# The up projection of a ConvFFN as seven block products instead of eight, in a pass of its own

## Chip, core and metric

The kernel runs on one core of a Trainium2 chip. The metric is the device time of one execution in microseconds (us): 2776.97 us is the median of three runs before the change (2772.65 to 2777.08).

## What is computed

One layer over 512 latent tokens and 256 context tokens, width 2048: sandwich norms, a token mixer (mLSTM heads and differential attention) and a gated ConvFFN. The change sits in the ConvFFN, whose hidden width is 5632:

```python
def dwconv3(a, w, b):
    ap = jnp.pad(a, ((0, 0), (1, 1), (0, 0)))
    return ap[:, :-2] * w[0] + ap[:, 1:-1] * w[1] + ap[:, 2:] * w[2] + b

def conv_ffn(h, w_up, conv_w, conv_b, w_down):
    u = dwconv3(h @ w_up, conv_w, conv_b)
    gate, val = jnp.split(u, 2, axis=-1)
    return (jax.nn.silu(gate) * val) @ w_down

h_lat = modulate(rmsnorm(x, g_pre_ffn[l]), sh2, sc2)
x = x + ga2 * rmsnorm(conv_ffn(h_lat, ...), g_post_ffn[l])
```

`h` is 512 x 2048, `w_up` 2048 x 11264, `w_down` 5632 x 2048, all in float32.

## The kernel before, in words

Every large product is done in three passes on rounded operands. `split` (L127) makes `hi` (a copy rounded to fp32r, on ScalarE) and `lo` (source minus `hi`, on VectorE); `mm3` (L131) adds hi·hi, hi·lo and lo·hi in PSUM. Weights stream from DRAM through `load_w` (L100): each 128 x 2048 weight tile comes in two 512 KB transfers to `raw` (three buffers), and is split in four pieces of 512 columns into `whi`/`wlo` (four buffers each).

Up projection: `up(m)` (L1013) computes one tile of 128 hidden columns for all 512 tokens: 16 blocks of the inner dimension times three passes, 48 matmuls of 512 columns, weights stationary, the normalized tokens (`hhi`, `hlo`) moving. `up(2f)` is the gate, `up(2f+1)` the value of hidden tile f; 44 tiles f in all. `conv3` (L570) evaluates the width-3 convolution (one ScalarE and two VectorE operations), ScalarE does the SiLU, VectorE the product.

Down projection: after every four tiles f, `nat_group` (L886) multiplies the four gated tiles (split into `fhi`, `flo`) with 512 rows of `w_down` and adds the result to the 16 accumulators `y` on VectorE: 192 matmuls of 512 columns a group, 11 groups. The last group goes through `nat_last` (L891), one token block at a time, each followed by its norm and output (`post`).

Between the mixer and the FFN stands a transition (L976 to L1000): the last group of the mixer's output projection gives `y` token block by token block, `post` normalizes it, TensorE transposes it (`xt`), ScalarE modulates it into `hf`, and VectorE writes `hhi` (L999) and `hlo` (L1000). Half of the first up tile (256 tokens) is computed early, inside the transition.

`step` (L341) does a slice of the conditioning product (`wmB` weights against a vector, on VectorE, and 8 matmuls of one column named `modr` per 512 outputs); the FFN calls it 16 times.

The program is written in the order of the stages; a scheduler places each engine's instructions, and each engine then runs its own list in order. SP issues the loads from DRAM, POOL the stores to it.

Of the kernel before, what the change touches and what calls it, by code (L numbers as in the profile page):

```python
# [6 lines left out]
F32 = mybir.dt.float32  # L7
F32R = mybir.dt.float32r
AF = mybir.ActivationFunctionType
ALU = mybir.AluOpType  # L10
# [4 lines left out]
P = 128  # L15
D = 2048
KT = 16
TL = 512
# [4 lines left out]
NFF = DFF // P  # L23
# [35 lines left out]
class Prog:  # L59
# [7 lines left out]
    def mm(self, *a, **k):  # L67
        return self.pe(self.nc.tensor.matmul(*a, **k))  # L68
# [28 lines left out]
    def slot(self, name, dt=F32):  # L97
        return self.p_slot.tile([P, 512], dt, tag="slot", name=name)

    def load_w(self, src, n, act=False):  # L100

        his, los = [], []
        if act:
            bh, bl = self.act("wact"), self.act("wact")
        for j in range(n // 512):
# [16 lines left out]
        return get  # L122

    def act(self, name):
        return self.p_act.tile([P, 4, 512], F32R, tag="act", name=name)

# [4 lines left out]
    def mm3(self, ps, whi, wlo, ahi, alo, start, stop):  # L131
        mm = self.mm
        mm(ps, whi, ahi, start=start, stop=False)
        mm(ps, whi, alo, start=False, stop=False)
        mm(ps, wlo, ahi, start=False, stop=stop)


    def setup(self, ctx):
# [744 lines left out]
        else:  # L883
            nc.vector.tensor_tensor(y[tt][cc], ps, y[tt][cc], ALU.add)  # L884

    def nat_group(self, wsrc, acts, y, first, pool, tag):  # L886
# [21 lines left out]
        self.nc.scalar.activation(self.junk5(), t, AF.Square, accum_out=ss[:, cc:cc + 1])  # L908

    def junk5(self):  # L910
        return self.p_x.tile([P, 512], F32, tag="junk5", name="junk5", bufs=2)

    def stat_done(self, ss):
        r = self.p_s.tile([P, 1], F32, tag="rs1", name="rs1")
# [4 lines left out]
    def load_row(self, g):  # L919
        out = []  # L920
        for cc in range(4):
            t = self.p_x.tile([P, 512], F32, tag="row", name="row", bufs=4)
            self.nc.sync.dma_start(t, self.gg_d[g:g + 1, cc * 512:(cc + 1) * 512].broadcast_to([P, 512]))
            out.append(t)
        return out

    def new_ss(self):
        return self.p_s.tile([P, 4], F32, tag="ss4", name="ss4", bufs=4)
# [16 lines left out]
    def phase_out(self):  # L945
        nc, I = self.nc, self.I
        y = self.y
        self.x1_d = self.dram.tile([4, P, D], F32, name="x1_d")
        rows = []
        acts = self.mix_acts(3)  # L950
        ssy = [self.new_ss() for _ in range(4)]

        def each(tt, cc):
            self.stat(ssy[tt], cc, y[tt][cc])
            nc.vector.tensor_tensor(y[tt][cc], y[tt][cc], rows[cc], ALU.mult)  # L955

        def post(tt):
            r = self.stat_done(ssy[tt])
            ss = self.p_s.tile([P, 4], F32, tag="ssx", name="ssx")
            xs = []  # L960
            for cc in range(4):
                xn = self.p_x.tile([P, 512], F32, tag="xn", name="xn", bufs=8)
                cs = slice(cc * 512, (cc + 1) * 512)
                nc.sync.dma_start(xn, I["xn"][tt, :, cs])
# [12 lines left out]
        self.nat_last(lambda cc: I["wo"][cc, 3], acts, y, self.ps_mm, "mm", 3, each, post)  # L977
        self.ah = [self.act("hhi") for _ in range(4)]
        self.al = [self.act("hlo") for _ in range(4)]
        for tt in range(4):  # L980
            if tt == 2:
                self.early = self.up_mm(0, 0, 256)
            ts = slice(tt * P, (tt + 1) * P)
            for cc in range(4):
# [6 lines left out]
                hf = self.p_x.tile([P, 512], F32, tag="hf", name="hf", bufs=4)  # L991
                for j in range(4):
                    k = cc * 4 + j
                    js = slice(j * P, (j + 1) * P)
                    sh, sc = self.mcol[:, 16 + k:17 + k], self.mcol[:, 32 + k:33 + k]
                    nc.scalar.activation(hf[:, js], pt[:, js], AF.Identity, bias=sh, scale=sc)  # L996
                h3 = hf.rearrange("p (a b) -> p a b", b=P)
# [5 lines left out]
    def up_mm(self, m, t0, t1, part=None):  # L1003

        if part is None:
            part = (self.load_w(self.I["wu"][m], 2048), self.ps_mm.tile([P, 512], F32, tag="mm", name="mm"))
        get, ps = part
        for kt in range(KT):
            hi, lo = self.hl(kt)
            self.mm3(ps[:, t0:t1], *get(kt * P, P), hi[:, t0:t1], lo[:, t0:t1], kt == 0, kt == KT - 1)  # L1010
        return part

    def up(self, m):  # L1013
        ps = (self.up_mm(m, 256, TL, self.early) if m == 0 else self.up_mm(m, 0, TL))[1]
        u = self.p_x.tile([P, 512], F32, tag="u", name="u", bufs=4)
        c = self.cff.rearrange("p (a b) -> p a b", b=4)
        self.conv3(u, ps, c[:, m, :], TL)
        if m >= 12:
            self.step(64)
        return u  # L1020

    def phase_ffn(self):
        nc, I = self.nc, self.I
# [8 lines left out]
        def post(tt):  # L1032
            r = self.stat_done(ssy[tt])
            for cc in range(4):
# [3 lines left out]
                nc.vector.scalar_tensor_tensor(x1, y[tt][cc], r, x1, ALU.mult, ALU.add)  # L1038
                nc.sync.dma_start(self.out[tt, :, cs], x1)

        NG = NFF // 4
        for g in range(NG):
            acts = ([], [])
            for j in range(4):
                f = g * 4 + j
# [4 lines left out]
                hi = self.slot("fhi", F32R)  # L1050
                lo = self.slot("flo", F32R)
                self.split(hi, lo, u)
                acts[0].append(hi)
                acts[1].append(lo)
            if g == NG - 1:
                rows += self.load_row(1)
                self.nat_last(lambda cc: I["wd"][g, cc], acts, y, self.ps_sm, "sm", 4, each, post)
            else:
                self.nat_group(lambda cc: I["wd"][g, cc], acts, y, g == 0, self.ps_sm, "sm")

    def build(self):
        with ExitStack() as ctx:
            self.setup(ctx)
            self.phase_in()
            self.p_x = ctx.enter_context(self.tc.tile_pool(name="ext", bufs=2))
            self.cff = self.p_x.tile([P, 88 * 4], F32, name="cff", bufs=1)
            self.nc.sync.dma_start(self.cff, self.I["cff"])
            self.phase_out()
            self.phase_ffn()
# [100 lines left out]
```

## Time and profile before

| | us |
|---|---|
| median of three runs | 2776.97 |
| the profiled execution's own time | 2775.6 |
| its span (first to last instruction) | 2773.8 |
| end of the last VectorE statement chain of the mixer's output (last `xn`) | 1309.83 |
| up and down products without a break on TensorE | from 1325.46 |

A span is the time from the first to the last instruction of the trace; the execution's own time is 1.8 us longer. Engine names: PE is TensorE, PEld its weight loads, DVE VectorE, ACT ScalarE, POOL GpSimd, SP the queue that issues loads. A matmul's own duration in the trace holds its way through the array, which overlaps with its successor; the cost of one in a stream is the distance between two starts.

### The profile page before, as it was taken

The numbers are of one execution on the slowest core, as the hardware profiler recorded it, in microseconds if no ns is written. First come the engines' busy times: TensorE is split into PE (matmuls) and PEld (weight loads), VectorE is DVE, ScalarE is ACT, GpSimd is POOL, SyncE is SP. The second block draws the span as 40 slices with busy tenths as digits, with TensorE's granted clock in tenths as the row PEclk, the third lists the DMA queues.
The fourth block names the chain that finished last, engine by engine and source line by source line (L and its number), as shares of the span: only waits on it lengthen the run. The fifth ranks groups of instructions, "written<-read, shape, count | busy, mean of one in ns | idle before, by whom it ended". The sixth has DMA issues, their size and how long they took to land.

```text
span 2773.8 us, 35993 instructions
## 1 busy us (share of the span) xinstructions
PE 2714.9 (98%) x13796; PEld 2263.1 (82%) x13796; DVE 1603.4 (58%) x2938; ACT 1012.5 (37%) x1939; POOL 78.7 (3%) x101
## 2 busy tenths in 40 slices
PE   6999999999999999998999999999999999999998
PEld 3678899888888888887888888888888888888886
DVE  6585867776666666457535565544444444444446
ACT  4242444434334344526433232323232322323233
POOL 0000000000000000002000000000000000000000
PEclk9999999999999999999999999999999999999999
DMA  7875434333433433334224354422222232222225
GB/s 277 272 245 194 134 115 134 134 125 114 130 129 126 136 119 130 133 115 143 99 97 141 127 190 137 144 96 94 99 95 97 90 106 92 99 99 99 92 99 174
DMA packets 111963, 365.46 MB, mean 132 GB/s; under 512 B 12896, under 2 KB 13312, under 8 KB 111792
## 3 DMA queue, kind: packets, MB, share of 16 engines
q1 hardware_dynamic: 108144, 352.03, 37.9%
q0 software_dynamic: 3648, 11.14, 1.1%
q8 instruction: 108, 1.77, 0.3%
q14 instruction: 63, 0.52, 0.1%
HBM read 348.36 MB, written 14.76 MB: 131 GB/s over the span
## 4 chain that ended last, share of the span: by engine, by line
PE 51%; DVE 2%; ACT 1%; issue 0%; DMA 0%; POOL 0%; POOLq 0%; DVEq 0%; ACTq 0%
PE mm L68 34%; PE nat L68 16%; ACT junk L908 0%; DVE x L1038 0%; DVE y L884 0%; DVE y L1030 0%; DVE xn L965 0%; DMA raw<-in_wd 0%; POOL rs L174 0%; ACT hf L996 0%; DVE hlo L1000 0%; DVE wact L129 0%; DVE y L955 0%; PE modr L68 0%; ACT y L972 0%
## 5 line engine op out<-in xcount | busy, mean ns | idle before, releaser
L128 ACT CAST whi<-raw 128x512 fp32r<-128x512 f32 x792 | 490.0, 622 | 1149.7 <-PE mm L68 600.7
L129 DVE TENSOR_TENSOR wlo<-raw,whi 128x512 fp32r<-128x512 f32 x792 | 542.9, 689 | 602.0 <-ACT whi L128 597.5
L68 PE MATMUL mm<-hhi,whi 128*128 128x512 f32 (+1 forms) x1424 | 552.2, 388 | 3.8 <-DVE hhi L999 3.8
L68 PE MATMUL mm<-hhi,wlo 128*128 128x512 f32 (+1 forms) x1424 | 551.7, 387 | 0.8 <-DVE wlo L129 0.8
L68 PE MATMUL mm<-hlo,whi 128*128 128x512 f32 (+1 forms) x1424 | 551.8, 387 | 0.5 <-DVE hlo L1000 0.3
L68 PE MATMUL mm<-lhi,whi 128*128 128x512 f32 x912 | 373.4, 410 | 1.7 <-ACT whi L128 1.4
L68 PE MATMUL mm<-llo,whi 128*128 128x512 f32 x912 | 360.2, 395 | 0.0
L68 PE MATMUL mm<-lhi,wlo 128*128 128x512 f32 x912 | 359.9, 395 | 0.0
L68 PEld LDWEIGHTS mm<-hhi,whi 128*128 128x128 f32 x1424 | 268.0, 188 | 58.6 <-DVE hhi L999 4.2
L68 PEld LDWEIGHTS mm<-hhi,wlo 128*128 128x128 f32 x1424 | 268.0, 188 | 55.3 <-DVE wlo L129 1.0
L68 PEld LDWEIGHTS mm<-hlo,whi 128*128 128x128 f32 x1424 | 268.0, 188 | 54.9 <-DVE hlo L1000 1.0
L68 PE MATMUL nat<-whi,flo 128*128 128x512 f32 x640 | 249.7, 390 | 0.0
L68 PE MATMUL nat<-wlo,fhi 128*128 128x512 f32 x640 | 249.5, 390 | 0.0
L68 PE MATMUL nat<-whi,fhi 128*128 128x512 f32 x640 | 248.8, 391 | 0.0
L884 DVE TENSOR_TENSOR y<-nat,y 128x512 f32<-128x512 f32 x208 | 141.9, 688 | 179.5 <-PE nat L68 179.3
L254 DVE SCALAR_TENSOR_TENSOR macc<-raw,c,macc 128x512 f32<-128x512 f32 x240 | 179.5, 748 | 103.0 <-DMA raw<-in_wmB 100.2
L68 PEld LDWEIGHTS mm<-lhi,wlo 128*128 128x128 f32 x912 | 172.5, 189 | 42.0 <-issue 2.9
L68 PEld LDWEIGHTS mm<-lhi,whi 128*128 128x128 f32 x912 | 173.3, 190 | 40.5 <-issue 9.9
L68 PE MATMUL cx<-chl,whi 128*128 128x256 f32 x1056 | 199.0, 287 | 0.5 <-ACT vt L612 0.3
L68 PEld LDWEIGHTS mm<-llo,whi 128*128 128x128 f32 x912 | 173.3, 190 | 30.5 <-issue 3.7
L68 PEld LDWEIGHTS cx<-chl,whi 128*128 128x128 f32 x1056 | 169.4, 191 | 7.5 <-ACT vt L612 0.8
L68 PE MATMUL cx<-chl,wlo 128*128 128x256 f32 x528 | 149.6, 283 | 0.0
(301 smaller groups left out, 3111.0 us busy)
## 6 DMA issues: line engine op xcount, KB each, us to landing
raw<-in_wu SPq DMA_DIRECT2D x176, 512.0 KB, 3.6
raw<-in_wmB SPq DMA_DIRECT2D x128, 512.0 KB, 4.0
raw<-in_w SPq DMA_DIRECT2D x105, 512.0 KB, 4.0
raw<-in_wd SPq DMA_DIRECT2D x88, 512.0 KB, 3.6
mraw<-in_wmA SPq DMA_DIRECT2D x64, 512.0 KB, 5.3
raw<-in_wo SPq DMA_DIRECT2D x32, 512.0 KB, 3.8
row<-row_d SPq DMA_DIRECT2D x32, 256.0 KB, 4.2
raw<-in_w SPq DMA_DIRECT2D x18, 256.0 KB, 3.5
```

The source lines that it names most:

```text
L68: return self.pe(self.nc.tensor.matmul(*a, **k))
L128: self.nc.scalar.copy(hi, src)
L129: self.nc.vector.tensor_tensor(lo, src, hi.bitcast(F32), ALU.subtract)
L254: nc.vector.scalar_tensor_tensor(acc, r, c, acc, ALU.mult, ALU.add)
L884: nc.vector.tensor_tensor(y[tt][cc], ps, y[tt][cc], ALU.add)
```

## The change

The 512 x 2048 token matrix is cut in four blocks (token halves 1 and 2, halves of the inner dimension 1 and 2): A11, A12, A21, A22. For each tile f the weights are four blocks: gate upper half B11, gate lower half B21, value upper half B12, value lower half B22. Seven products with sums of blocks (Winograd's form of Strassen's scheme, S1 to S4 on the token side) replace the eight block products. Each product has 8 blocks of the inner dimension times three passes, 24 matmuls of 256 columns.

- The token-side sums S1 to S4 and the splits of A11, A12, A22 and S1 to S4 are made once, in the transition (`put_form`, `sums`).
- The weight-side sums are made per f: B12 + B11 and B12 + B22 by a load and a second, adding load of the same tile from POOL (`forms`); two more sums on VectorE (L1168, L1176).
- The up projection of all 44 tiles runs first. The gated product goes to DRAM (`g_d`), and the down projection reads it back four tiles at a time (`down_acts`).
- Every second weight block is split in one piece of 1024 columns into a new pair of buffers (`vhi`, `vlo`); the down projection does so too. The 16 `step` calls move from the up tiles to the down groups.
- The buffers `hf`, `xn`, `junk5` and `row` move into shared pools (`F`, `u`, `raw`, `slots`).

```diff
@@ nat_group
-            get = self.load_w(wsrc(cc), 2048)
+            get = self.load_w(wsrc(cc), 2048, wide=down and cc % 2 == 1)
+            if down and cc % 2 == 0:
+                self.step(64)
@@ phase_out, transition
-        self.ah = [self.act("hhi") for _ in range(4)]
-        self.al = [self.act("hlo") for _ in range(4)]
+        self.forms(0)
+        for n in ("A11", "A12", "A22"):
+            self.fm[n] = [[self.slot(n, F32R) for _ in range(4)] for _ in range(2)]
...
-                hi, lo = self.ah[cc][:, :, ts], self.al[cc][:, :, ts]
-                nc.vector.tensor_copy(hi, h3)
-                nc.vector.tensor_tensor(lo, h3, hi.bitcast(F32), ALU.subtract)
+                if tt < 2:
+                    self.put_form("A11" if cc < 2 else "A12", cc % 2, tt, h, True)
+            if tt >= 2:
+                self.sums(tt, hf)
+            if tt == 2:
+                self.early = [self.up_first(0)]
+            if tt == 3:
+                self.early.append(self.up_first(1))
...
+    def sums(self, tt, hf):
+        tt_ = self.nc.vector.tensor_tensor
...
+        for c in range(2):
+            tt_(s1[c], s1[c], hf[tt - 2, c], ALU.subtract)
+            self.put_form("S2", c, tt, s1[c])
...
+    def forms(self, f):
+        g, v = self.I["wu"][2 * f], self.I["wu"][2 * f + 1]
+        for b in (g[:, :1024], v[:, 1024:]):
+            t = self.f_tile("F")
+            nc.sync.dma_start(t, v[:, :1024])
+            nc.gpsimd.dma_start(t, b, accum_op=ALU.add)
...
+    def weight(self, t):
+        self.nwt += 1
+        if self.nwt % 2:
+            hi, lo = self.wide_w()
+            self.split(hi, lo, t)
...
+        for q in range(2):
+            hi = self.p_w.tile([P, 512], F32R, tag="whi", name="whi")
+            lo = self.p_w.tile([P, 512], F32R, tag="wlo", name="wlo")
+            self.split(hi, lo, t[:, q * 512:(q + 1) * 512])
...
+    def up_p1(self, f):
+        b1 = self.up_ps(self.ps_mm, "mm")
+        gate = self.slot("gate")
+        self.prod(b1, "A11", self.weight(self.raw_w(self.I["wu"][2 * f, :, :1024])), True)
+        self.nc.scalar.copy(gate[:, :256], b1)
+        return b1, gate
+
+    def up_p2(self, f, gate, r21):
+        b3 = self.up_ps(self.ps_sm, "sm")
+        self.prod(b3, "A12", self.weight(r21), True)
+        self.nc.vector.tensor_tensor(gate[:, :256], b3, gate[:, :256], ALU.add)
...
+    def up(self, f):
...
+        if f + 1 < NFF:
+            self.forms(f + 1)
+        b1, gate, r21 = self.early[f] if early else (*self.up_p1(f), None)
+        F, F3 = self.fl.pop(f)
...
+        self.prod(b2, "S1", self.weight(F), True)
+        nc.scalar.copy(c22, b2)
+        r22 = self.raw_w(wu[2 * f + 1, :, 1024:])
+        tt_(F, F, r22, ALU.add)
+        self.prod(b1, "S2", self.weight(F), False)
+        nc.scalar.activation(c12, b1, AF.Copy, scale=-1.0)
+        if not early:
+            r21 = self.raw_w(wu[2 * f, :, 1024:])
+            self.up_p2(f, gate, r21)
+        self.prod(b1, "S3", self.weight(F3), False)
+        tt_(c22, c22, b1, ALU.subtract)
+        tt_(F, F, r21, ALU.add)
+        self.prod(b2, "S4", self.weight(r22), False)
+        tt_(c12, b2, c12, ALU.add)
+        self.prod(b1, "A22", self.weight(F), False)
+        nc.scalar.copy(c21, b1)
+        self.conv3(v, val, c[:, 2 * f + 1, :], TL)
+        self.conv3(u, gate, c[:, 2 * f, :], TL)
+        nc.scalar.activation(u, u, AF.Silu)
+        tt_(u, u, v, ALU.mult)
+        nc.gpsimd.dma_start(self.g_d[f], u)
@@ phase_ffn
+        for f in range(NFF):
+            self.up(f)
+        nxt = self.down_acts(0)
         for g in range(NG):
-            for j in range(4):
-                u = self.up(2 * f)
-                nc.scalar.activation(u, u, AF.Silu)
-                v = self.up(2 * f + 1)
-                nc.vector.tensor_tensor(u, u, v, ALU.mult)
-                self.split(hi, lo, u)
+            acts = nxt
+            if g < NG - 1:
+                nxt = self.down_acts(g + 1)
```

How the change stands in the engines' lists is shown at two places. First VectorE in the middle of the up projection. Before, these rows are one tile f (gate and value); `wlo` is a weight split, L573 and L574 the convolution, L1049 the gated product, `flo` the split for the down projection:

```order
L129 TENSOR_TENSOR wlo<-raw,whi 128x512
L129 TENSOR_TENSOR flo<-u,fhi 128x512
L129 TENSOR_TENSOR wlo<-raw,whi 128x512 x3
L573 SCALAR_TENSOR_TENSOR u<-mm,cff,u 128x511
L574 SCALAR_TENSOR_TENSOR u<-mm,cff,u 128x511
L129 TENSOR_TENSOR wlo<-raw,whi 128x512 x4
L573 SCALAR_TENSOR_TENSOR u<-mm,cff,u 128x511
L574 SCALAR_TENSOR_TENSOR u<-mm,cff,u 128x511
L1049 TENSOR_TENSOR u<-u 128x512
```

Now, a part of one tile f; `up` is a product in PSUM, so L1146, L1175 and L1178 wait for TensorE (the ends of A12, S3 and S4), L1168 and L1176 are the two weight sums, `vlo` a weight split of 1024 columns:

```order
L1146 TENSOR_TENSOR gate<-up,gate 128x256
L144 TENSOR_TENSOR wlo<-raw,whi 128x512
L1175 TENSOR_TENSOR val<-val,up 128x256
L144 TENSOR_TENSOR vlo<-F,vhi 128x1024
L1168 TENSOR_TENSOR F<-F,raw 128x1024
L1178 TENSOR_TENSOR val<-up,val 128x256
L144 TENSOR_TENSOR wlo<-F,whi 128x512
L588 SCALAR_TENSOR_TENSOR v<-val,cff,v 128x511
L144 TENSOR_TENSOR wlo<-F,whi 128x512
L589 SCALAR_TENSOR_TENSOR v<-val,cff,v 128x511
L1176 TENSOR_TENSOR F<-F,raw 128x1024
L588 SCALAR_TENSOR_TENSOR u<-gate,cff,u 128x511
```

The weight splits, the sums of weights and the work on finished products now alternate in one list. Second, VectorE at the end of the transition. Before, the last token block's last two pieces close it:

```order
L999 CAST hhi<-hf 128x4x128
L1000 TENSOR_TENSOR hlo<-hf,hhi 128x4x128
L999 CAST hhi<-hf 128x4x128
L1000 TENSOR_TENSOR hlo<-hf,hhi 128x4x128
L129 TENSOR_TENSOR wlo<-raw,whi 128x512 x4
```

Now the sums and splits of the last token block (S2: L1079, S3: L1083, S4: L1086, splits L1068) stand ahead of the weight split L144 of the first S2 product:

```order
L1086 TENSOR_TENSOR s_12643<-s_12643,hf 128x512
L1068 TENSOR_TENSOR S_12455<-s_12639,S_12454 128x4x128
L1068 TENSOR_TENSOR A_12336<-hf,A_12332 128x2x128
L1068 TENSOR_TENSOR S_12455<-s_12643,S_12454 128x4x128
L1068 TENSOR_TENSOR A_12337<-hf,A_12333 128x2x128
L1068 TENSOR_TENSOR A_12338<-hf,A_12334 128x2x128
L1068 TENSOR_TENSOR A_12339<-hf,A_12335 128x2x128
L1146 TENSOR_TENSOR gate<-up,gate 128x256
L144 TENSOR_TENSOR wlo<-F,whi 128x512 x2
```

From the mixer's last `xn` (L990, before L965) up to and with the first of these two weight splits the list of VectorE now holds 91 instructions: 16 casts of 256 columns and 4 of 512, 26 two-operand operations of 256 columns, 37 of 512 and 4 of 1024, 2 scalings of 512 and 2 of one column.

## Rows read from the trace of the kernel before

**Rows 1.** Page: the span, and busy time by engine.
```profile
span 2773.8 us, 35993 instructions
PE 2714.9 (98%) x13796; PEld 2263.1 (82%) x13796; DVE 1603.4 (58%) x2938; ACT 1012.5 (37%) x1939; POOL 78.7 (3%) x101
```

**Rows 2.** Chain of waits that ended last: start us, us, what.
```profile
1307.76 2.07 DVE xn L965 x3
...
1325.46 82.08 PE mm L68 x383
1407.54 43.80 PE nat L68 x192
1451.34 87.04 PE mm L68 x384
1538.38 0.79 PE modr L68 x8
...
2632.02 78.67 PE mm L68 x347
```

**Rows 3.** Timeline, TensorE and one VectorE row: start us, us, what [idle before].
```profile
1295.51 1.28 DVE L884 TENSOR_TENSOR y<-nat,y 128x512 f32<-128x512 f32 x2
...
1317.75 0.28 PE L68 MATMUL mm<-hhi,whi 128*128 128x256 f32 x1
...
1321.58 0.28 PE L68 MATMUL mm<-hhi,wlo 128*128 128x256 f32 x1
...
1339.83 0.39 PE L68 MATMUL mm<-hhi,wlo 128*128 128x512 f32 x1
...
1344.82 0.39 PE L68 MATMUL mm<-hhi,whi 128*128 128x512 f32 x1
...
2725.61 1.45 PE L68 MATMUL nat<-wact,fhi 128*128 128x512 f32 x5 [1.57 <-ACT fhi L128]
```

**Rows 4.** Groups by line and form, VectorE: count | busy us, mean ns | idle before.
```profile
L129 DVE TENSOR_TENSOR wlo<-raw,whi 128x512 fp32r<-128x512 f32 x792 | 542.9, 689 | 602.0 <-ACT whi L128 597.5 <-PE vtp L71 1.8 <-DMA xn<-in_xn 0.7
...
L573 DVE SCALAR_TENSOR_TENSOR u<-mm,cff,u 128x511 f32<-128x511 f32 x88 | 65.9, 749 | 0.0
...
L760 DVE TENSOR_TENSOR kb<-dk,kb 64x768 fp32r<-64x768 f32 x16 | 15.2, 953 | 1.1 <-ACT kb L759 0.5
...
L999 DVE CAST hhi<-hf 128x512 fp32r<-128x512 f32 x16 | 6.8, 425 | 2.7 <-ACT hf L996 2.7
...
L231 DVE TENSOR_TENSOR cT<-cT,rcrrb 128x256 f32<-128x256 f32 x16 | 6.2, 418 | 0.0
...
L974 DVE TENSOR_SCALAR y<-xn,rs 128x512 f32<-128x512 f32 x8 | 3.5, 484 | 2.4 <-POOL rs L174 2.4
```

**Rows 5.** Groups by line and form, ScalarE.
```profile
L128 ACT CAST whi<-raw 128x512 fp32r<-128x512 f32 x792 | 490.0, 622 | 1149.7 <-PE mm L68 600.7 <-PE nat L68 312.8 <-PE cx L68 98.4
...
L759 ACT CAST kb<-dk 64x768 fp32r<-64x768 f32 x16 | 13.3, 832 | 14.3 <-DVE den L707 7.2 <-DVE dk L733 6.9
...
L612 ACT COPY vt<-cx 128x256 f32<-128x256 f32 x16 | 5.8, 365 | 0.0
...
L572 ACT ACTIVATE q<-acc,cw 128x512 f32<-128x512 f32 x4 | 3.3, 817 | 0.0
```

**Rows 6.** Windows: stretch, length, busy of each engine, clock, DMA share, GB/s.
```profile
1309.84:1325.46 15.62, 12.56 (x78) 10.92 (x78) 12.78 (x25) 15.40 (x44) 1.53 (x3) 0.81 0.35 120
2239.65:2326.69 87.04, 87.04 (x386) 72.10 (x385) 37.67 (x55) 28.87 (x47) 0.00 (x0) 1.00 0.30 103
```

**Rows 7.** Page: DMA queues (packets, MB, share of 16 engines), and one load.
```profile
q1 hardware_dynamic: 108144, 352.03, 37.9%
q0 software_dynamic: 3648, 11.14, 1.1%
q8 instruction: 108, 1.77, 0.3%
...
raw<-in_wu SPq DMA_DIRECT2D x176, 512.0 KB, 3.6
```

More of the change, by code (lines that the diff above doesn't have):

```diff
@@ L104, in load_w @@
             bh, bl = self.act("wact"), self.act("wact")
+        if wide:
+            for j in range(n // 1024):
+                raw = self.p_raw.tile([P, 1024], F32, tag="raw", name="raw")
+                self.nc.sync.dma_start(raw, src[:, j * 1024:(j + 1) * 1024])
+                hi, lo = self.wide_w()
+                self.split(hi, lo, raw)
+                for q in range(2):
+                    his.append(hi[:, q * 512:(q + 1) * 512])
+                    los.append(lo[:, q * 512:(q + 1) * 512])
+            n = 0
         for j in range(n // 512):
@@ L122, in load_w, with wide_w @@
         return get
+    def wide_w(self):
+        hi = self.p_x.tile([P, 1024], F32R, tag="vhi", name="vhi")
+        lo = self.p_x.tile([P, 1024], F32R, tag="vlo", name="vlo")
+        return hi, lo
     def act(self, name):
@@ L910, in junk5 @@
     def junk5(self):
-        return self.p_x.tile([P, 512], F32, tag="junk5", name="junk5", bufs=2)
+        return self.slot("junk5")
     def stat_done(self, ss):
@@ L921, in load_row @@
         for cc in range(4):
-            t = self.p_x.tile([P, 512], F32, tag="row", name="row", bufs=4)
+            t = self.u_tile("row")
             self.nc.sync.dma_start(t, self.gg_d[g:g + 1, cc * 512:(cc + 1) * 512].broadcast_to([P, 512]))
@@ new lines, in phase_out, with put_form @@
+            if tt >= 2:
+                self.sums(tt, hf)
[3 more added lines that the diff above has]
+                self.early.append(self.up_first(1))
+    def put_form(self, n, c, tt, src, on_dve=False):
+        nc = self.nc
+        h3 = src.rearrange("p (a b) -> p a b", b=P)
+        t0 = tt % 2 * P
+        hi, lo = self.fm[n]
+        if n[0] == "S":
+            parts = [(h3, *(t.rearrange("p a (b t) -> p (a b) t", b=2)[:, 4 * c:4 * c + 4, t0:t0 + P]
+                            for t in (hi, lo)))]
+        else:
+            parts = [(h3[:, 2 * q:2 * q + 2, :],
+                      *(t[2 * c + q].rearrange("p (b t) -> p b t", b=2)[:, :, t0:t0 + P] for t in (hi, lo)))
+                     for q in range(2)]
+        for s, h, l in parts:
+            if on_dve:
+                nc.vector.tensor_copy(h, s)
+            else:
+                nc.scalar.copy(h, s)
+            nc.vector.tensor_tensor(l, s, h.bitcast(F32), ALU.subtract)
@@ new lines, in sums @@
+    def sums(self, tt, hf):
+        tt_ = self.nc.vector.tensor_tensor
+        s1 = []
+        for c in range(2):
+            s = self.slot("s1")
+            s1.append(s)
+            tt_(s, hf[tt, c], hf[tt, c + 2], ALU.subtract)
+            self.put_form("S1", c, tt, s, True)
+        for c in range(2):
+            tt_(s1[c], s1[c], hf[tt - 2, c], ALU.subtract)
+            self.put_form("S2", c, tt, s1[c])
+        for c in range(2):
+            a = hf[tt, c]
+            tt_(a, hf[tt - 2, c], a, ALU.subtract)
+            self.put_form("S3", c, tt, a)
+        for c in range(2):
+            tt_(s1[c], s1[c], hf[tt - 2, c + 2], ALU.add)
+            self.put_form("S4", c, tt, s1[c])
+        for c in range(2):
+            self.put_form("A22", c, tt, hf[tt, c + 2])
@@ new lines, in weight @@
+    def weight(self, t):
+        self.nwt += 1
+        if self.nwt % 2:
+            hi, lo = self.wide_w()
+            self.split(hi, lo, t)
+            return [(hi[:, i * P:(i + 1) * P], lo[:, i * P:(i + 1) * P]) for i in range(8)]
+        out = []
+        for q in range(2):
+            hi = self.p_w.tile([P, 512], F32R, tag="whi", name="whi")
+            lo = self.p_w.tile([P, 512], F32R, tag="wlo", name="wlo")
+            self.split(hi, lo, t[:, q * 512:(q + 1) * 512])
+            out += [(hi[:, i * P:(i + 1) * P], lo[:, i * P:(i + 1) * P]) for i in range(4)]
+        return out
@@ new lines, in prod, with up_ps @@
+    def prod(self, ps, n, w, first):
+        hi, lo = self.fm[n]
+        for i in range(8):
+            a, b = i // 2, slice(i % 2 * 256, i % 2 * 256 + 256)
+            if n[0] == "S":
+                h, l = hi[:, a, b], lo[:, a, b]
+            else:
+                h, l = hi[a][:, b], lo[a][:, b]
+            self.mm3(ps, *w[i], h, l, first and i == 0, i == 7, skip_group_check=True)
+    def up_ps(self, pool, tag):
+        return pool.tile([P, 512], F32, tag=tag, name="up")[:, :256]
+    def up_p1(self, f):
[4 more added lines that the diff above has]
+        return b1, gate
@@ new lines, in down_acts @@
+    def down_acts(self, g):
+        last = g == NFF // 4 - 1
+        if last:
+            his = [self.slot("fhi", F32R) for _ in range(4)]
+            los = [self.slot("flo", F32R) for _ in range(4)]
+        else:
+            hi, lo = self.act("ghi"), self.act("glo")
+            his = [hi[:, j, :] for j in range(4)]
+            los = [lo[:, j, :] for j in range(4)]
+        for q in range(2):
+            t = self.f_tile("gr")
+            t3 = t.rearrange("p (a t) -> p a t", a=2)
+            self.nc.sync.dma_start(t3, self.g_d[4 * g + 2 * q:4 * g + 2 * q + 2].rearrange("a p t -> p a t"))
+            if last:
+                for j in range(2):
+                    self.split(his[2 * q + j], los[2 * q + j], t[:, j * 512:(j + 1) * 512])
+            else:
+                self.split(hi[:, 2 * q:2 * q + 2, :], lo[:, 2 * q:2 * q + 2, :], t3)
+        return his, los
@@ L1058, in phase_ffn @@
             else:
[L1059 removed]
+                self.nat_group(lambda cc: I["wd"][g, cc], acts, y, g == 0, self.ps_sm, "sm", True)
     def build(self):
```

85 lines of the change are left out of this document (50 added, 35 removed).

## The prediction, written before the changed kernel ran

> **What bounds the kernel now.** First the busy table: TensorE is busy 98% of the span, VectorE 58%, ScalarE 37% [rows 1]. That a busy share says little about a pipelined engine is settled by the chain of waits: from 1325.46 us it is TensorE alone, `mm` pieces (up) and `nat` pieces (down) in turn, 384 matmuls in 87.04 us and 192 in 43.80, with nothing between them but four `modr` pieces of 0.79 us [rows 2]. So in the FFN a change is worth what it takes from TensorE's stream, as long as the engines that feed it keep pace. The window over one group of up tiles shows how much room they have: VectorE 37.67 and ScalarE 28.87 of 87.04 us, DMA 0.30 [rows 6]. Third, the timeline gives the pitch, the distance of two starts: 22 steps of 512 columns from 1339.83 to 1344.82, or 226.8 ns; 32 steps of 256 columns from 1317.75 to 1321.58, or 119.7 ns [rows 3]. Half the columns cost more than half.
>
> The time before, in parts that I use below: the up products from 1325.46 on are 87 whole tiles (4176 matmuls of 512 columns at 87.04/384 = 226.7 ns) and half of one (48 of 256 columns at 119.7), together 952 us; ten down groups at 43.76 and four `modr` make 441; that puts the start of the last group at 2719, and the tail to the end of the span at 2773.8 is 54.7 us. In the tail TensorE stands still once, 1.57 us before 2725.61, for the last `fhi` [rows 3].
>
> **The products.** Now 44 tiles x 7 products x 24 = 7392 matmuls of 256 columns. At 119.7 ns one tile f costs 168 x 0.1197 = 20.1 us (before 96 x 0.2267 = 21.8), the whole 885 against 958. One eighth of the columns goes (120 us), but the fixed 6.3 ns that 119.7 has over half of 226.8 is paid 7392 times and takes 47 back: 73 are left.
> Of this term the Trainium skill has a rule too. It gives a back-to-back distance of columns/2.4 GHz plus 2.5 ns (TensorE: Matmul & The Clock Gate, section Back-to-back issue gap), by which the saving would be an estimated 104 us, and the same section warns that the weight load also enters the distance in a stream of load and matmul pairs. The trace sides with the warning: 119.7 and 226.8 ns where the formula has 109 and 216.
>
> **Who feeds it.** Per tile f VectorE now has 3.5 weight splits of 1024 columns, 7 of 512, 2 weight sums of 1024, 3 operations of 256 on finished products, 4 of the convolution and the gated product. 512 columns take 0.689, 256 take 0.418, 768 take 0.953 [rows 4]; 1024 is not in the trace: between 0.953 and two of 512 (1.38), and the slope of 1.03 ns a column puts it at 1.22, which I take. Sum: 4.3 + 4.8 + 2.4 + 1.3 + 3.0 + 0.7 = 16.5 us of 20.1 (15.0 to 17.3 by the bounds). ScalarE: 3.5 casts of 1024 (1.05 by the same slope from 0.622 and 0.832), 7 of 512, 4 copies of 256 (0.365), 2 convolution starts (0.82), one SiLU (as a cast, 0.62): 11.7 us [rows 5]. Both fit. What stalls is order: L1146, L1175 and L1178 wait for a product, and the splits behind them wait too. But the two buffer pairs hold four products, so a split is due some three products (8.6 us) after its buffer comes free. In the tightest slot, A22, VectorE has 4.5 us of work in a product of 2.9; the 1.6 us of lag are worked off two products later. I cost this at nothing; when the cover is gone, each microsecond a tile is 43 us.
>
> **DMA.** Per tile seven transfers of 512 KB and one of 256: 3.9 MB in 20.1 us. The hardware queue moved 352 MB in 37.9% of the span, so 335 GB/s while it was at work, and the plain POOL queue 365 [rows 7]; that is 11.7 us of 20.1. Two of the seven add into what is there. No row shows an adding transfer. Lower bound: as plain. Upper bound from rows: the slowest queue of the page, q8, at 213 GB/s, 1.6 times the plain time. I take twice, since it reads two operands for each write: 14.9 us of 20.1, hidden. A pair is loaded more than one tile ahead, so its latency does not count, only the rate. The store and reload of the gated products (256 KB a tile, then 1 MB a group) lie in the same slack; in the down phase the DMA share was 0.26 to 0.30.
> The Trainium skill says that transfers issued from SP, ACT and POOL run on the same 16 DMA engines and interleave (DMA: Bandwidth & Descriptors, section Issuing engines are not separate DMA queues); that speaks against the adding loads, which cannot hide in a queue of their own. The page's shares fit it as one pool, and the sum above is made that way.
>
> **The transition.** This is where time is added. From the last `xn` (1309.83) VectorE now has 91 instructions up to the weight split of the first S2 product: 37 of 512 (0.689) 25.5, 26 of 256 (0.418) 10.9, 4 of 1024 4.9, 16 casts of 256 at some 0.28 (between 0.14 and 0.425) 4.5, 4 casts of 512 1.7, 2 scalings 1.0, small ones 0.3: 48.8 us, so 1358.6. Two that don't depend on each other follow in 1.28 instead of 1.38 [rows 3], which takes up to 3.4 off; ScalarE, busy 15.40 of 15.62 us there already [rows 6], puts some waits in. I take 1360. TensorE has by then done the A11 and A12 products of tiles 0 and 1 and the first S1 product (120 matmuls), and then stands; after such a standstill it resumes at the lower of its two clock levels, 1.2 GHz (mean grant 0.81 in this stretch before, [rows 6]), some 2 us for the first S2 product. So the stream of 7272 matmuls, 870.5 us, starts in effect at 1362.
>
> **From up to down, and the end.** At the switch, the last quarter of the first down weights waits for the buffers of the last product and stands in VectorE's list behind a convolution step that needs the last product too: about copy 0.37, convolution start 0.82, 0.75, split 0.69, after which TensorE has 2.0 us of earlier pieces: 1.5 us lost (0 to 5). The down groups keep their pitch: VectorE gets the same weight splits, 16 additions and, in eight of them, the `wmB` steps. In the last group nothing waits for a last tile any more: the 1.57 us go, the tail is 53.1.
>
> **Sum.** 1362 + 870.5 + 441 + 1.5 + 53.1 = 2728 for the span, 45.8 less than 2773.8. With the 1.8 us around the span 2729.8; the median of the runs is 1.4 above the profiled execution: 2731.
>
> **Rivals.**
> 1. The adding loads bind (slower). The plain part of a tile takes 8.6 us of the DMA engines, so an adding transfer of 512 KB may take 5.75 us before DMA passes 20.1: 3.7 times the plain 1.57. From 4 times on (21.1 us a tile, +44) the gain is gone; at 5 times a tile takes 24.3 and the time is 2731 + 43 x 4.2 = 2910. For it: nothing in the trace shows such a transfer, and the load lies on one pool. Against: no queue of the page is slower than 1.6 times.
> 2. VectorE's list costs TensorE 0.5 to 1.3 us a tile: 2752 to 2787. For it: 82% busy, in order, with three waits on products a tile, and the `r22` load (3.6 us to land when the DMA engines are at 0.30) is issued only some 7 us before the sum that needs it. Against: three products of lead.
> 3. The transition is shorter: if VectorE runs at the 0.64 us pitch and the S2 split comes at 1350, and the switch is free, 2718 or less.
>
> **Chances.** The forecast (2712 to 2752) 0.62; rival 3, below that, 0.08; rival 2 0.14, of which 0.10 is still faster, 0.03 no change, 0.01 slower; rival 1 0.16, nearly all slower. A measurement tells 0.2% from no change, so faster means below 2771.4. Faster 0.80, same 0.04, slower 0.16. The range that holds 8 in 10 leaves out the lower edge of rival 3 and most of rival 1: 2708 to 2785; the forecast's own is 2712 to 2752.
>
> **What would show it.** Right: in the chain of waits one `up` stretch of about 870 us from about 1362, 24 matmuls in 2.87 us, then `nat` groups of 43.76; VectorE near 82% and ScalarE near 58% in the up window, DMA share near 0.7; the first S2 split of VectorE near 1360. Wrong: gaps on TensorE in the up window released by `wlo`/`vlo` (rival 2) or by F's adding load, with a DMA share near 1 (rival 1); or a pitch of 256 columns above 125 ns, which would cost 39 us.

## The result and the profile after

The changed kernel takes 2742.85 us (median of four runs, 2741.49 to 2743.70) against 2776.38 of before (also four runs now, one more than stood above): ratio 0.9881, 95% interval 0.9864 to 0.9899, so 1.2% faster. The forecast was 2731 us, in the range 2708 to 2785; the result also lies in the forecast's own range, 2712 to 2752. The profiled execution took 2743.7 us.

From the profile's page: the span, busy time by engine, the two large queues, and the loads of the up projection (count, size, median us from issue to landing). Against [rows 1, 7], q0 has grown from 11 to 69 MB.

```profile
span 2741.9 us, 43239 instructions
PE 2652.5 (97%) x16916; PEld 2355.4 (86%) x16916; DVE 1887.8 (69%) x3252; ACT 1192.8 (44%) x2185; POOL 178.6 (7%) x233
q1 hardware_dynamic: 119312, 386.64, 43.0%
q0 software_dynamic: 19840, 68.83, 11.8%
raw<-in_wu SPq DMA_DIRECT2D x132, 512.0 KB, 5.3
F<-in_wu SPq DMA_DIRECT2D x88, 512.0 KB, 5.0
F<-in_wu POOLq DMA_DIRECT2D x88, 512.0 KB, 7.6
```

The chain of waits (start us, us, what) of the same execution, to compare with [rows 2]:

```profile
1360.86 0.60 DVE S L1068
...
1364.94 0.61 DVE wlo L144
...
1365.60 2.52 PE up L68 x10
...
1368.44 9.41 DMA raw<-in_wu
...
1390.08 837.84 PE up L68 x7053
...
2230.73 6.32 DMA raw<-in_wmB
...
2239.22 65.14 PE nat L68 x281
2304.36 0.79 PE modr L68 x8
2305.14 88.61 PE nat L68 x384
...
2574.17 1.13 DVE vlo L144
2575.30 0.08 DVE mcol L286
2575.38 0.04 issue
2575.43 0.28 PE modr L71
2575.70 155.80 PE nat L68 x672
```

The up projection is one stretch of TensorE, as forecast, but three places now have other work in the chain: the begin of the stream (1365 to 1390), the switch to `nat` at 2235, and a stop at 2575 before a transposition. Two down groups take 88.61 us between their `modr`, where one of [rows 2] took 43.80.

The windows (length, busy of PE, PEld, DVE, ACT, POOL; clock, DMA share, GB/s) show the transition, the begin of the stream, and the rest of the up pass:

```profile
1309.00:1365.60 56.60, 35.77 (x210) 30.44 (x208) 52.16 (x112) 48.80 (x121) 6.97 (x12) 0.81 0.40 128
1365.60:1390.08 24.48, 21.64 (x156) 20.95 (x156) 17.36 (x23) 11.05 (x18) 4.01 (x5) 0.88 0.84 208
1390.08:2227.90 837.82, 837.82 (x7055) 837.82 (x7056) 653.67 (x865) 468.67 (x740) 93.55 (x123) 1.00 0.74 198
```

In the third TensorE never stands still, VectorE is busy 78%, ScalarE 56%, DMA 0.74. The transition is VectorE's: busy 52.16 of 56.60 us. But this window holds more than the forecast's list of 91 instructions. That list starts at the mixer's last `xn`, which ended at 1309.83 us before [rows 2]. Now it ends at 1322.62 (a row of TensorE and one of VectorE; in brackets: idle us, releaser):

```profile
1185.23 0.79 PE L68 MATMUL nat<-whi,mhi 128*128 128x512 f32 x1 [5.52 <-DVE y L899]
...
1319.88 2.74 DVE L990 SCALAR_TENSOR_TENSOR xn<-y,rs,xn 128x512 f32<-128x512 f32 x4 [0.72 <-POOL rs L189]
```

So the mixer, whose arithmetic the change leaves alone, ends 12.8 us later, and the list itself takes 42.9 us to the end of its first split at 1365.55, with VectorE busy for 41.98. In the experiments with the whole change the last `xn` ends between 1320.2 and 1326.4 us, in the one that has the mixer of before (experiment 1) at 1309.3. Half of the delay is there when TensorE starts the mixer's output projection, at 1113.0 us instead of 1106.6. Up to this point every engine runs the same instructions in the same order in both kernels; the time goes in small steps between 500 and 900 us, and why is open. The stop at 1185 comes on top: the addition that TensorE waits for stands in VectorE's list behind splits that wait, through ScalarE, for the loads of `mixr`. These take 8.9 us to land there (from 1165 to 1192 us), and 5.4 before. The change has put the first loads of `forms(0)` there; that they are the reason is not shown.

The timeline of TensorE has the pitch (distance of two block starts): up blocks of 24 matmuls from narrow, wide, narrow weight pieces, then down blocks of 48 from wide, narrow, wide.

```profile
1502.41 0.40 PE L68 MATMUL up<-S,whi 128*128 128x256 f32 x2
...
1505.28 0.40 PE L68 MATMUL up<-A,vhi 128*128 128x256 f32 x2
...
1508.11 0.40 PE L68 MATMUL up<-S,whi 128*128 128x256 f32 x2
...
2405.43 0.40 PE L68 MATMUL nat<-vhi,ghi 128*128 128x512 f32 x1
...
2416.64 0.40 PE L68 MATMUL nat<-whi,ghi 128*128 128x512 f32 x1
...
2427.55 0.40 PE L68 MATMUL nat<-vhi,ghi 128*128 128x512 f32 x1
```

An up block takes 2.87 us from `whi` (119.6 ns a matmul) and 2.83 from `vhi` (117.9). A down block takes 11.21 us from `vhi` and 10.91 from `whi`: the wide pieces, which the change brought, are slower where they are the moving operand (the one that streams past the stationary weights of the array). Four more rows of TensorE end in a wait (in brackets: idle us, releaser):

```profile
1365.60 0.58 PE L68 MATMUL up<-S,wlo 128*128 128x256 f32 x1 [2.30 <-DVE wlo L144]
...
1390.08 0.51 PE L68 MATMUL up<-S,whi 128*128 128x256 f32 x2 [1.80 <-ACT val L1170]
...
2238.11 0.51 PE L68 MATMUL nat<-whi,ghi 128*128 128x512 f32 x1 [1.69 <-ACT whi L143]
...
2575.43 0.28 PE L71 MATMUL modr<-tabs,mcol 128*16 128x128 f32 x1 [2.08 <-DVE mcol L286]
```

### The profile page after: what moved, and what is told of

Read it like the earlier page. It is cut to its first block, busy times and chain, and to the rows that moved or that the text cites. A ratio compares the mean times of both kernels' runs of the same rounds, so it can differ in the third digit from the quotient of the medians.

```text
span 2741.9 us, 43239 instructions
## 1 busy us (share of the span) xinstructions
PE 2652.5 (97%) x16916; PEld 2355.4 (86%) x16916; DVE 1887.8 (69%) x3252; ACT 1192.8 (44%) x2185; POOL 178.6 (7%) x233
## 4 chain that ended last, share of the span: by engine, by line
PE 49%; DVE 1%; ACT 1%; DMA 1%; issue 0%; DVEq 0%; POOLq 0%; POOL 0%; ACTq 0%
PE up L68 31%; PE nat L68 18%; ACT hf L1032 1%; DMA raw<-in_wu 0%; DMA raw<-in_wmB 0%; DVE S L1068 0%; DVE vlo L144 0%; ACT junk L925 0%; ACT vhi L143 0%; DVE wlo L144 0%; PE xt L71 0%; PE modr L68 0%; ACT S L1067 0%; DVE A L1068 0%; DVE v L588 0%
## 5 line engine op out<-in xcount | busy, mean ns | idle before, releaser
L143 ACT CAST whi<-raw 128x512 fp32r<-128x512 f32 x492 | 302.8, 620 | 455.4 <-PE nat L68 174.6
L144 DVE TENSOR_TENSOR wlo<-raw,whi 128x512 fp32r<-128x512 f32 x492 | 337.4, 692 | 105.9 <-ACT whi L143 99.0
L68 PE MATMUL up<-S,whi 128*128 128x256 f32 x1408 | 259.3, 284 | 5.4 <-ACT S L1067 3.1
L68 PE MATMUL up<-S,vhi 128*128 128x256 f32 x1408 | 253.8, 281 | 1.0 <-ACT val L1166 0.9
L68 PEld LDWEIGHTS up<-S,whi 128*128 128x128 f32 x1408 | 220.0, 192 | 6.1 <-ACT S L1067 3.3
L68 PEld LDWEIGHTS up<-S,vhi 128*128 128x128 f32 x1408 | 215.5, 188 | 1.5 <-ACT val L1166 1.1
L68 PE MATMUL up<-S,wlo 128*128 128x256 f32 x704 | 200.1, 284 | 2.3 <-DVE wlo L144 2.3
L143 ACT CAST vhi<-raw 128x1024 fp32r<-128x1024 f32 x106 | 111.3, 1050 | 199.8 <-PE nat L68 154.8
L68 PE MATMUL up<-S,vlo 128*128 128x256 f32 x704 | 197.0, 280 | 0.0
L68 PE MATMUL up<-A,vhi 128*128 128x256 f32 x1056 | 192.9, 283 | 0.1
L68 PE MATMUL up<-A,whi 128*128 128x256 f32 x1056 | 192.8, 283 | 0.0
L144 DVE TENSOR_TENSOR vlo<-raw,vhi 128x1024 fp32r<-128x1024 f32 x106 | 129.6, 1223 | 53.8 <-ACT vhi L143 53.6
```

## The experiments

Ten kernels ran, each timed in turn with the kernel before. A ratio is to the kernel before, with its 95% interval; the changed kernel's is 0.9881.

**1. One part alone: the pass without the seven products.** The kernel before, with all up tiles first and the gated products through DRAM:

```diff
+        for f in range(NFF):
+            u = self.up(2 * f)
+            nc.scalar.activation(u, u, AF.Silu)
+            v = self.up(2 * f + 1)
+            nc.vector.tensor_tensor(u, u, v, ALU.mult)
+            nc.gpsimd.dma_start(self.g_d[f], u)
...
+        nxt = self.down_acts(0)
         for g in range(NG):
-            acts = ([], [])
-            for j in range(4):
...
+            acts = nxt
```

> The kernel before with one part of the change: all up tiles first, the gated products through DRAM to the down projection; eight products in 512-column matmuls, the transition, the weight pieces and the place of the step calls as before. Theory 'the seven products bring the gain': the pass alone is worth what the end of the stream saves (1.57 us in the tail) less a switch of 1 to 3 us: 2774 to 2780, so that the products with their transition bring the other 31 to 37 us. Rival 'the pass brings it' (fewer changes between up and down): 2745 to 2760.

Measured: 2788.98 us, ratio 1.0049 [1.0030, 1.0067]. Neither theory had it slower by that much. The `step` calls now follow one another from up tile to up tile, and VectorE waits for their loads (row of the waits from 1560 to 1640 us: us in total, times, longest):

```profile
DVE macc L254 <- DMA raw<-in_wmB: 27.3, 11, 4.4
```

TensorE's own waits from 1330 us on add up to 6.9 us, nearly all for weight pieces, here and around the down groups, where before had 1.57. That is some 5 of the 11 us by which this kernel is slower; the rest stays open. So the order of work is not where the gain is: the products, with the transition, the wide weight pieces and the other places for the steps, bring 2789 - 2743 = 46 us, although the mixer ends later with them.

**2. VectorE's cover (rival 2 of the prediction).** Five more additions a tile f:

```diff
+        def extra(F):
+            t = self.p_x.tile([P, 512], F32, tag="extra", name="extra", bufs=1)
+            tt_(t, F[:, :512], F[:, 512:], ALU.add)
...
         self.prod(b2, "S1", self.weight(F), True)
+        extra(F)
```

The other four calls stand behind the products S2, S3, S4 and A22.

> Five more VectorE additions of 512 columns in each up tile f, into a buffer that nothing reads: 5 x 0.69 = 3.4 us a tile on VectorE, which is busy 653.67 of 837.8 us in the up stretch now, 15.5 of 19.9 us a tile; with them 18.9, 95%. Theory 'VectorE's list is covered by three products of lead': TensorE still does not wait in the up stretch or only in a few places, 2743 to 2752. Rival 'in order, with three waits a tile, the cover ends before the busy share reaches 100%': 1 to 3.4 us a tile, 2787 to 2890.

Measured: 2738.97 us, ratio 0.9861 [0.9846, 0.9876]. The same stretch of the up pass:

```profile
1390.08:2227.90 837.82, 837.82 (x7058) 837.82 (x7057) 771.69 (x1076) 468.12 (x738) 93.63 (x123) 1.00 0.74 199
```

VectorE is at 92% and TensorE still never waits: the cover is real. That the kernel became some 4 us faster (the two intervals overlap) was expected by neither. In its trace the last transposition of the transition stands 1.6 us earlier, from there to the last up matmul it is 1.7 us less, and from there to the last group 2.5 less. Of the 1.6 us 1.5 are there at the mixer's last `xn` already. Whether the rest comes from another order of VectorE's list was not tried.

**3. The adding loads (rival 1).** Each sum added twice, so that F is B12 + 2 B11 and B12 + 2 B22:

```diff
-            nc.gpsimd.dma_start(t, b, accum_op=ALU.add)
+            self.tc.keep_in_program_order(nc.gpsimd.dma_start(t, b, accum_op=ALU.add))
             out.append(t)
+        for t, b in zip(out, (g[:, :1024], v[:, 1024:])):
+            self.tc.keep_in_program_order(nc.gpsimd.dma_start(t, b, accum_op=ALU.add))
```

The edit also holds these loads to the order of the program. The changed kernel's POOL list has that order by itself (2082.48 us the store, then the two adding loads at 2086.39 and 2091.94, then the next store), so what is new is the second pair.

> Each of the two weight sums by adding load is added twice (F holds B12 + 2 B11 and B12 + 2 B22), so a tile f has four adding loads instead of two. In the changed kernel the DMA share of the up stretch is 0.74 of 19.04 x 44 us, 14.7 us a tile; 5 plain loads and a store take 5.5 x 1.57 = 8.6, so an adding load takes 3.05. Theory 'adding loads cost twice a plain one, and are hidden': with four, 20.8 us a tile against TensorE's 19.9, so DMA becomes the bound: share near 1 in the up stretch, TensorE waits for F, the time rises by about 0.9 x 43 = 40 us to 2780. Rival 'they cost no more than a plain one and the share counts something else': 17.8 us a tile, still hidden, 2743. Rival 'far dearer when they crowd': over 2850.

Measured: 3176.4 us, ratio 1.1436 [1.1419, 1.1453], 10 us a tile. The number is the third theory's, but not its mechanism. A long window of the up pass, POOL's rows of one tile, and the page's q0:

```profile
1420.00:2600.00 1180.00, 932.15 (x6571) 905.81 (x6570) 601.26 (x803) 414.64 (x684) 158.29 (x195) 0.86 0.67 166
```

```profile
2082.15 1.79 POOL L1099 DMA_DIRECT2D F<-in_wu  x2
...
2112.19 0.58 POOL L1189 DMA_DIRECT2D g_d<-u  x1 [14.57 <-DVE u L1188]
2112.75 1.78 POOL L1099 DMA_DIRECT2D F<-in_wu  x2
2123.11 0.86 POOL L1102 DMA_DIRECT2D F<-in_wu  x1 [8.58 <-DMA F<-in_wu]
```

```profile
q0 software_dynamic: 32512, 114.97, 17.5%
```

The DMA engines are busy 0.67, less than before, so they do not bind. POOL's list does: first adds, a wait for their landing, second adds, and then the store, which waits for the tile's end; the next first adds come 30.6 us after the last. In this window TensorE waits 247.8 us, 6.4 a tile; the other 4 us a tile are its own matmuls, slower at a mean granted clock of 0.86. From q0, the extra 46.1 MB took 556.1 - 323.5 = 232.6 us of all engines, or 2.64 us for an adding load of 512 KB, 1.7 times the plain 1.57. Against experiment 1, whose POOL queue has the same stores and no adding loads, the changed kernel's 46.1 MB more take 323.5 - 61.3 us, or 2.98 a load, 1.9 times:

```profile
q0 software_dynamic: 7168, 22.68, 2.2%
```

So a second run added a load that lengthens no chain:

```diff
+        nc.vector.tensor_copy(self.junk_f[:, :1], u[:, :1])
+        nc.gpsimd.dma_start(self.junk_f, wu[2 * f, :, :768], accum_op=ALU.add)
...
+            self.junk_f = self.p_x.tile([P, 768], F32, name="junk_f", bufs=1)
```

> From the changed kernel: one more adding load a tile f, of 768 columns, into a buffer that nothing else reads, issued after the store of the gated product. It adds DMA work (0.75 of an adding load) but no step to the chain base load, adding load, use. In the run with every sum added twice the extra 46.1 MB took 232.6 us of the 16 engines (q0 556.1 against 323.5 us), 2.64 us an adding load, so here 2.0 us a tile: DMA share of the up stretch 0.74 to 0.84. Theory 'what cost 10 us a tile there was the longer chain, not the rate': no cost here, within 4 us of the changed kernel (2739 to 2747), TensorE without waits in the up stretch. Rival 'adding loads slow down when there are more of them': 0.75/2 of the 10 us a tile, 3.8 x 43 = 160 us more, 2900.

Measured: 2747.34 us, ratio 0.9879 [0.9863, 0.9896]: no cost against the changed kernel's ratio. The window:

```profile
1390.08:2227.90 837.82, 836.02 (x7041) 835.82 (x7040) 655.00 (x907) 468.17 (x739) 132.15 (x167) 1.00 0.84 217
```

The share is the 0.84 expected; from the last transposition to the last up matmul it is 883.5 us, against 883.7 in the changed kernel. The rate of the added load is hidden, so what the sums added twice had to pay was one more landing in POOL's ordered list. A run with the store in another queue, which would part the landing from the order, was not made.

**4. The wide pieces of the down projection.** The table `cff` 32 bytes longer, the list of every engine unchanged:

```diff
-            self.cff = self.p_x.tile([P, 88 * 4], F32, name="cff", bufs=1)
+            self.cff = self.p_x.tile([P, 88 * 4 + 8], F32, name="cff", bufs=1)[:, :352]
```

> The question is why the down products from the wide weight pieces (vhi, vlo) stand 233.4 ns apart and those from whi, wlo 227.4. The table cff is allocated 32 bytes longer, so that every buffer behind it starts 32 bytes later; in the changed kernel vhi and vlo start at a multiple of 64 bytes, whi and wlo 32 bytes past one. The order of the instructions is the same. Theory 'place': the moving operand's start decides, so the wide pieces fall to 227.4 ns and the time by 20 x 48 x 6.0 ns = 5.8 us, to about 2737; the up products from wide pieces, 117.9 ns now, may then move to the 119.6 of the narrow ones, which gives 44 x 84 x 1.7 ns = 6 us back, so about 2743 in all. Theory 'form': a piece of a 1024-column buffer is dearer wherever it starts: 233.4 and 117.9 ns stay, 2743.

Measured: 2741.16 us, ratio 0.9867 [0.9850, 0.9883]; that alone could not be told from the changed kernel, but its chain can:

```profile
2305.76 87.81 PE nat L68 x384
2393.58 0.79 PE modr L68 x8
2394.36 87.81 PE nat L68 x384
```

Two groups take 87.81 instead of 88.61 us, so a wide matmul 4.2 ns less; the up blocks stay at 2.83 and 2.88. The shift explains 4.2 of some 6 ns in the down products and nothing in the up products. But it moved the narrow pieces by 32 bytes as well, and their mean distance in the down groups did not change (228.2 ns before the shift, 228.0 after), so the place of the start alone is not the reason either. The other side, no wide pieces in the down projection:

```diff
-            get = self.load_w(wsrc(cc), 2048, wide=down and cc % 2 == 1)
+            get = self.load_w(wsrc(cc), 2048)
```

> From the changed kernel: the down projection splits all its weights in pieces of 512 columns (whi, wlo), none in vhi, vlo; the buffers stand where they stood. The shift by 32 bytes had taken 4.2 of the 6.0 ns by which wide pieces are slower. Theory 'the rest is the form': all down products at 227.4 ns, 20 x 48 x 6.0 = 5.8 us less, 2737, if four buffer pairs feed TensorE as eight did. Rival 'half the buffers, so new waits': TensorE waits for whi or wlo in the down groups and the time is 2743 or more.

Measured: 2794.81 us, ratio 1.0051 [1.0035, 1.0068]: the rival, and far above its bound of 2743. TensorE's waits in the down pass:

```profile
PE nat L68 <- DVE wlo L144: 20.5, 14, 2.5
PE modr L68 <- DVE macc L269: 20.5, 4, 5.3
```

The stretch from the first down product to the last group is 504.3 us instead of 452.9; TensorE waits 44.1 us in it, where the changed kernel has 4.4, and the mean granted clock is 0.96. Between the waits the pitch is 227.3 ns, so the narrow form is the faster one. But the buffers `vhi`, `vlo` are what lets the down groups take the `wmB` steps: with four pairs of 512 columns alone the splits, and the steps' loads through the same three `raw` buffers, come too late. The waits end with the steps: from 2631 us, behind the last `modr`, to 2733 us TensorE waits for nothing, with the same four pairs.

**5. The three stops.** The early tiles load r21 again, instead of holding two of three `raw` buffers:

```diff
-        if not early:
-            r21 = self.raw_w(wu[2 * f, :, 1024:])
-            self.up_p2(f, gate, r21)
+        r21 = self.raw_w(wu[2 * f, :, 1024:])
+        if not early:
+            self.up_p2(f, gate, r21)
```

> From the changed kernel: the two early tiles load their gate lower half (r21) a second time when the sum needs it, instead of holding two of the three raw buffers through the transition. Theory 'held buffers': the load of raw that VectorE waits 9.41 us for at 1368.44 is issued late because the buffers are held; without that, the 144 matmuls after 1365.60, 24.48 us instead of 17.1, lose at most 3 us: 4 to 5 us off, 2738. Rival 'VectorE's and ScalarE's own lists' (splits of the last sums still running beside the first weight splits, clock 0.88): the stretch stays near 24 us, 2743.

Measured: 2739.06 us, ratio 0.9860 [0.9846, 0.9875]. The window as long as the one of 24.48 us above, and the row with the last wait of the up pass:

```profile
1367.30:1391.80 24.50, 23.93 (x186) 23.55 (x187) 20.04 (x27) 13.10 (x20) 4.66 (x6) 0.94 0.94 242
```

```profile
1372.42 0.51 PE L68 MATMUL up<-S,vhi 128*128 128x256 f32 x2 [0.56 <-ACT val L1170]
```

186 matmul records instead of 156, and the waits at 1386 and 1390 are gone. From the last transposition to the end of up: 3.7 us less. So the held buffers caused these two waits. The expectation's 144 matmuls and 17.1 us are a miscount (see the terms below), and its 9.41 us are the load's flight, of which VectorE waited 2.90. With a third early tile on top (`self.early.append(self.up_first(2))`, its sum in a PSUM buffer that is free then):

> The run with the second load of r21, and a third tile whose A11 and A12 products are computed in the transition (its sum stands in another PSUM buffer). TensorE is busy 35.8 of the 56.6 us of the transition, so there is room for 48 matmuls (5.7 us). Theory 'TensorE's spare time is to be had': VectorE, which is busy 52.2 of those 56.6 us, gets 2.6 us of weight splits more, so the stream ends 3 us earlier: 3 us below the run with the second load alone. Rival 'VectorE is the bound and its list grows': the first S2 split comes 2.6 us later and the waits for splits behind it grow as well, no gain (0 to 2 us above).

Measured: 2738.07 us, ratio 0.9847 [0.9828, 0.9865]. By the same milestones 1.1 us below the run without it: between theory and rival. TensorE now waits 5.58 us for a weight split before an early product (at 1363.79); this split stands at the end of VectorE's list of sums and splits, which has no gap from 1352 us on. The down projection, with the buffers 32 bytes later as in experiment 4:

```diff
-            if down and cc % 2 == 0:
+            if down and not first and cc % 2 == 0:
                 self.step(64)
             for tt in range(4):
+                if tt == 2 and self.row_due is not None:
+                    self.modb_row(self.row_due)
+                    self.row_due = None
...
+            self.cff = self.p_x.tile([P, 88 * 4 + 8], F32, name="cff", bufs=1)[:, :352]
```

> From the changed kernel, three edits of the down projection, each with its own place in the trace: the buffers 32 bytes later (as in the run with the shifted buffers), the transposition modb_row issued two units of 12 matmuls after the columns it needs, and the step calls from the second group on instead of the first. Theory: (a) wide pieces 229.2 ns, 4 us off; (b) the stall of 2.08 us before 2575.43, with the slow matmuls behind it 4.8 us, is TensorE waiting in its own order for mcol behind VectorE's weight splits, so it goes; (c) of the 2.3 us at the switch some 1 us is VectorE waiting for the first wmB load, and goes. Sum 8 to 10 us: 2733 to 2735. Rival for (b): TensorE waits there for the weight splits themselves, and stands still a few matmuls later: 4 us less of the gain. Rival for (c): the first convolution after the last product sets it, and the 2.3 us stay.

Measured: 2734.54 us, ratio 0.9844 [0.9829, 0.9859]. From the first `nat` to the last group 443.3 us against 452.9: 9.6 less, the sum expected. Its chain has nothing but TensorE there:

```profile
2527.29 87.81 PE nat L69 x384
2615.10 0.79 PE modr L69 x8
2615.89 5.57 PE nat L69 x24
2621.46 0.11 PE modr L72
2621.57 103.94 PE nat L69 x456
```

The 2.08 us before the transposition are gone, and the switch waits 0.45 us instead of 2.3; with 4.0 us from the shift that leaves some 4 for the transposition. All together:

> All edits of the other three together: second load of r21, third early tile, shifted buffers, late transposition, steps from the second group on. If they add up (4.5 + 3 + 9): 2726 to 2728. If the rivals hold (held buffers, third tile and switch worth nothing): 2735.

Measured: 2729.65 us (2728.86 to 2730.62), ratio 0.9824 [0.9810, 0.9839]: below both kernels, with intervals that do not meet the changed kernel's. By the milestones the up pass is 3.5 us shorter than in the changed kernel and the down pass 8.4, together 12 of the 16.5 that the parts were expected to give; another 1.6 are there at the last transposition of the transition. Its chain from the last wait of the up pass on:

```profile
1374.35 848.21 PE up L69 x7131
...
2232.89 108.96 PE nat L69 x474
```

## Why the prediction was right, and which terms were off

The sign and the mechanism held: TensorE's stream sets the time, and VectorE and DMA stay hidden. The 7392 matmuls at 118.8 ns are 878 us against the 958 of before; a later mixer, transition, begin of the stream and down groups take 48 of these 80 back. No up stretch from 1390.08 us on waits for VectorE's list or an adding load, so rivals 1 and 2 did not come. The span came out 13.9 us longer than the sum of 2728: the mixer 12.8, the begin of the stream 3.5, switch and down groups 10.4 and the tail 1.1 more, VectorE's list 7.2 and the products 6.6 less. So it is partly luck that the number is this near: two terms that came out better than counted hide most of the one that the sum did not have. By terms:

- **Products, 119.7 ns.** Right for narrow pieces (119.6); wide ones are at 117.9. Over the 7113 matmuls from 1390.08 to 2234.88 that is 118.8 ns, 6.6 us better than counted.
- **Who feeds it.** 78% and 56% where 82% and 58% stood, 1.22 and 1.05 us for 1024 columns as estimated (1223 ns and 1050 ns in the groups). Experiment 2 confirms the cover.
- **DMA.** Right in size (0.74 for 0.74): an adding load costs 1.7 to 1.9 plain ones where 2 stood. The sentence that the latency does not count is true only as POOL's list stands; experiment 3 shows what one more landing in that list costs.
- **Transition.** VectorE's list ended at 1365.6 and not 1360, by two errors that partly cancel. Its start, the mixer's last `xn`, was taken over from the trace of before and came 12.8 us later; the prediction has no term for a change to the mixer, although the change moves its buffers and starts the first loads of the sums inside it. The list itself took 42.9 us where 50.2 stood, mostly since its operations of 512 columns follow one another at 0.60 us and not at 0.69. That is the reason of rival 3: with the mixer of before the split would have come near 1353. The lower clock after the standstill was priced at 2 us and came: from 1365.60 to 1371.30 the granted clock is 0.50, and the 25 matmuls there take some 2.5 us more than at 119.7 ns.
- **Begin of the stream.** What I left out altogether: 155 matmuls took 24.48 us instead of 18.6, with the slower ones included, and 2.8 us of it are three waits. I asked whether VectorE and the DMA rate suffice, not which buffers are held: the early tiles kept two `raw` buffers, and a load that was issued when the first came free took 9.41 us to land, of which VectorE waited 2.90. By 1390.08 TensorE was 9.1 us behind the forecast; the faster pitch gave back all but 2.4.
- **Switch and down groups.** This is the term that was mis-sized most within the FFN: "The down groups keep their pitch". From the end of up to the last group it took 452.9 us where 441 + 1.5 stood. The wide pieces cost 20 x 0.30 = 6 us, the transposition at 2575 some 4 with the slow matmuls behind it (granted clock 0.59 from 2575.46 to 2579.65), the switch 0.8 more than counted. I had priced the wide split on VectorE, and not the same buffer as an operand of TensorE. And the steps moved next to a transposition that TensorE's list puts right behind VectorE's answer: in the up tiles of before no such wait showed (the only idle time there was the 1.57 us of [rows 3]). Experiment 5 takes 9.6 of the 10.4 us away.
- **Tail.** 54.2 for 53.1.

Not settled: why a start 32 bytes later makes the wide moving operand faster but not the narrow one, and what the other 2 ns are; why experiment 2 was faster; why the mixer ends 12.8 us later; half of what the pass alone cost in experiment 1.

## What to carry to other kernels

When a change brings a new buffer, price it at every engine that reads it, and list what each instruction holds until it ends: here early products that kept two load buffers cost 3.7 us, which no row of busy time showed. A queue that runs in order can fail by its order before its rate does, as POOL's did in experiment 3 with the DMA engines at 0.67, so look for a wait whose landing stands ahead of the next issue. And when a part moves to another stage, follow its small instructions too: a transposition of 0.28 us stopped TensorE for 2. Nor does a stage that the change seems to leave alone keep its end by itself: the mixer ended 12.8 us later, the largest term that the sum lacked.

## What was not expected of the hardware

- The moving operand's place: 512 columns from the wide buffers stand 233.5 ns apart, 229.4 when every buffer starts 32 bytes later, and 227.3 from narrow ones, whose distance the shift did not change. As stationary operand the wide buffers give the shorter distance (117.9 against 119.6 ns, 256 columns), and the shift changes nothing there.
- An adding load of 512 KB takes 2.64 to 2.98 us of the DMA engines by q0 (plain: 1.57 by [rows 7]) and 7.6 us to land where the plain one takes 5.0.
